# A two-layer hybrid decoder trunk: one plain group instead of three at the feed-forward's entry, two groups begun early, and other transfers at the start and the end

## The chip, the cores and the metric

The kernel runs on one core of a Trainium2 chip. The metric is the device time of one execution in microseconds (us), as the median of several runs. Before the change it is 2063.41 us (median of 3 runs, 2063.31 to 2064.4).

The core has five engines with a queue of instructions each: TensorE (PE) multiplies matrices, VectorE (DVE) and ScalarE (ACT) work on tiles, GpSimd (POOL) does elementwise work too, and SyncE (SP) issues transfers. An engine takes its queue strictly in the order in which the program was written out.

## What is computed

Two layers on a sequence of 1024 tokens with 1024 channels, all in float32. The feed-forward, where most of the change lies, is the second half of a layer:

```python
for l in range(DEPTH):
    h = rmsnorm(x, attn_norm[l])
    ...                                   # four token mixers on slices of h @ w_in[l]
    x = x + mixed @ w_o[l]
    h2 = rmsnorm(x, ffn_norm[l])
    gate, up = jnp.split(h2 @ w_gate_up[l], 2, axis=-1)
    x = x + (jax.nn.silu(gate) * up) @ w_down[l]
return rmsnorm(x, final_norm)
```

The inner width of the feed-forward is 2816, that is 22 groups of 128 gate columns and 128 up columns.

## The kernel before

**Products.** Activations are kept transposed, 128 channels by 512 tokens in a half tile (a "half" of a slot; two halves make a pair). The 1024 tokens are two halves, `HALVES = (1, 0)`. Each float32 operand is split into a high and a low part of type float32r: ACT copies the high part, DVE subtracts it (`split`, L281; `half_split`, L291; `pair_split`, L1114, on 1024 columns). A product of blocks is then three matmuls for each 128 channels: high by high, high by low, low by high (`mm3`, L267).

**The feed-forward.** Gate and up weights are one 2 by 2 block matrix for each group, the two token halves and the even and odd channel tiles the other. A plain group (`plain`, L1268) makes all eight products, four for each half `u`. A Strassen group makes seven, on combinations of the blocks: for the activations N1, N2, T3, T4 (`combine(j)`, L1054, for j = 0 to 3, made once for each layer), for the weights three sums that POOL makes (`GateUp.sums`, L1128) and a fourth (`sum4`, L1152). `GateUp(f)` (L1119) issues the two 512 KB loads of group `f`; `split1` to `split4` split its parts. `gu_start` (L1179) makes a Strassen group's first two products, on the blocks B11 and B21, which are plain parts of the input, and weights that are no sums. The other five need N2, N1, T3, B22 and T4 (`onto`, L1167, adds a product to a bank that holds one). `NPL = 3` groups are plain, 19 are Strassen groups (L1465 to L1535).

**The entry.** After the attention, `norm_a` (L1032) scales its outputs, `out_last(t, ma)` (L1084) adds the last quarter of the output projection for a token half, splits the result into B11 and B21 or B12 and B22, stores it and adds up its squares. `norm(u)` (L1423) makes the reciprocal root of a half's mean square (Ln, Exp and Square on ACT). The weights of groups 0 and 1 are loaded between the two halves of `out_last`. Then (L1426 to L1463) the six halves of plain groups alternate with the four calls of `combine`, the gates, silus and products of the plain groups, and the splits of group 3.

**The start and the end.** The parameters (`par`) are loaded by POOL (L131). `weights` (L203) loads a weight tile of 512 KB with SP and splits it. `enter(t)` (L362) loads x in blocks of 256 KB and splits each with a gain from `par`. At the end the last token half is finished in two passes of 256 columns: the last products, eviction (`evac`, L1566), sum of squares, `rnorm` (L326), and `finish` (L375), which multiplies by gain and norm in one DVE instruction and stores each of 8 tiles with SP (L384).

**The order.** The program text sets what depends on what. The order on each engine is then written out by a list scheduler (`arrange`, L1817) from estimated lengths (`length`, L1718) and a table of shifts (`MOVES`), which moves groups of instructions in rank; `order_engines` (L2015) fixes it. So a change of the text or of an estimate moves instructions in the whole program. PSUM banks have tags with fixed counts (`ps`, L177).

## Time and profile before

| | |
|---|---|
| median of 3 runs | 2063.41 us |
| the profiled execution's own time | 2062.8 us |
| its span, first to last instruction | 2061.0 us |
| mean granted clock of TensorE | 0.998 |
| DVE busy, share of the span | 75% |
| ACT busy | 47% |
| POOL busy | 28% |
| transferred | 289.76 MB, mean 141 GB/s |

A profile describes one execution. "Busy" is the time in which an engine worked; the groups give for each source line and operation the count, the busy time, the mean length of one in ns, and the idle time of the engine just before with what ended it ("<-DVE u L1050" is a DVE instruction on line 1050 that wrote a tile u). L272 is the helper that issues nearly all matmuls, L283 and L284 are the two halves of a split. Instructions of one engine overlap a little, so the lengths of instructions that follow each other add up to more than the time they take. The chain of waits follows the run back from its last instruction, at each step to what released it. A timeline row gives start, length and instruction, several alike as one row with a count.

### The profile page before, as it was taken

The numbers are of one execution on the slowest core, as the hardware profiler recorded it, in microseconds if no ns is written. First come the engines' busy times: TensorE is split into PE (matmuls) and PEld (weight loads), VectorE is DVE, ScalarE is ACT, GpSimd is POOL, SyncE is SP. The second block draws the span as 40 slices with busy tenths as digits, with TensorE's granted clock in tenths as the row PEclk, the third lists the DMA queues.
The fourth block names the chain that finished last, engine by engine and source line by source line (L and its number), as shares of the span: only waits on it lengthen the run. The fifth ranks groups of instructions, "written<-read, shape, count | busy, mean of one in ns | idle before, by whom it ended". The sixth has DMA issues, their size and how long they took to land.

```text
span 2061.0 us, 26301 instructions
## 1 busy us (share of the span) xinstructions
PE 2038.0 (99%) x9442; PEld 1680.9 (82%) x9442; DVE 1539.8 (75%) x2420; ACT 971.0 (47%) x1712; POOL 571.3 (28%) x453
## 2 busy tenths in 40 slices
PE   8999999999999999999999999999999999999997
PEld 6887888887888888888888878888888888888887
DVE  7888988976766767655656898878877677786555
ACT  7547556643333334444434576656433333354332
POOL 0000000047776775100000000000677677650000
PEclk9999999999999999999999999999999999999999
DMA  5110222324444446966411102233344444498652
GB/s 181 42 45 30 74 86 98 133 103 159 168 159 152 166 158 231 340 236 208 138 36 44 57 16 86 75 118 113 133 169 158 155 163 157 143 325 303 201 177 87
DMA packets 148819, 289.76 MB, mean 141 GB/s; under 512 B 12608, under 2 KB 72000, under 8 KB 148688
## 3 DMA queue, kind: packets, MB, share of 16 engines
q1 hardware_dynamic: 148656, 288.03, 40.5%
q8 instruction: 74, 1.21, 0.2%
q14 instruction: 57, 0.47, 0.1%
q0 software_dynamic: 32, 0.04, 0.0%
HBM read 204.66 MB, written 83.36 MB: 140 GB/s over the span
## 4 chain that ended last, share of the span: by engine, by line
PE 95%; DVE 2%; ACT 1%; DMA 1%; issue 1%; POOL 0%; DVEq 0%; SPq 0%; ACTq 0%; POOLq 0%
PE ps_mm L272 36%; PE ps_s L272 29%; PE ps_t L272 12%; PE ps_pv L272 8%; PE ps_pv L962 2%; PE ps_t L950 1%; PE ps_s L896 1%; PE ps_t L336 1%; PE ps_s L897 1%; PE ps_s L898 1%; PE ps_pv L572 1%; PE ps_mm L770 1%; PE ps_s L511 1%; DVE u L284 1%; PE ps_t L560 1%
## 5 line engine op out<-in xcount | busy, mean ns | idle before, releaser
L272 PE MATMUL ps_mm<-u,u 128*128 128x512 f32 (+1 forms) x3376 | 835.5, 389 | 1.4 <-DVE u L1001 1.2
L272 PEld LDWEIGHTS ps_mm<-u,u 128*128 128x128 f32 x3376 | 621.7, 188 | 126.6 <-issue 4.0
L272 PE MATMUL ps_s<-u,u 128*128 128x512 f32 x2672 | 636.0, 390 | 9.5 <-ACT u L286 7.4
L272 PEld LDWEIGHTS ps_s<-u,u 128*128 128x128 f32 x2672 | 501.6, 188 | 116.2 <-ACT u L286 7.4
L284 DVE TENSOR_TENSOR u<-u,u 128x1024 fp32r<-128x1024 f32 (+2 forms) x380 | 449.5, 1206 | 154.1 <-ACT u L283 118.9
L283 ACT CAST u<-u 128x1024 fp32r<-128x1024 f32 (+2 forms) x380 | 328.1, 888 | 480.4 <-PE ps_mm L272 192.8
L272 PE MATMUL ps_t<-u,u 128*128 128x512 f32 (+1 forms) x1212 | 284.1, 378 | 0.0
L272 PEld LDWEIGHTS ps_t<-u,u 128*128 128x128 f32 x1212 | 222.7, 188 | 43.0 <-issue 0.5
L959 POOL MEMSET u<- 128x128 f32 x32 | 5.9, 212 | 844.8 <-PE ps_mm L272 653.0
L1312 POOL TENSOR_TENSOR tp<-tp,u 128x512 f32<-128x512 f32 x88 | 144.1, 1639 | 231.6 <-ACT tp L1311 231.3
L161 POOL TENSOR_TENSOR u<-u 128x256 f32<-128x256 f32 x176 | 188.7, 1072 | 66.4 <-DVE u L284 30.5
L272 PE MATMUL ps_pv<-u,u 128*128 128x512 f32 x696 | 167.4, 389 | 0.4 <-ACT u L283 0.4
L272 PEld LDWEIGHTS ps_pv<-u,u 128*128 128x128 f32 x696 | 130.5, 188 | 28.1 <-ACT u L283 0.8
L1311 ACT ACTIVATE tp<-tp 128x512 f32<-128x512 f32 x88 | 55.5, 632 | 127.4 <-DVE tp L348 126.7
L1132 POOL TENSOR_TENSOR u<-u,u 128x512 f32<-128x512 f32 x38 | 66.9, 1761 | 140.9 <-ACT tp L1311 83.9
L286 ACT ACTIVATE u<-u,par 128x512 fp32r<-128x512 f32 x100 | 69.9, 717 | 58.0 <-DVE u L1577 18.6
L283 ACT CAST u<-ps_t 128x512 fp32r<-128x512 f32 (+4 forms) x136 | 65.1, 506 | 56.4 <-PE ps_t L950 32.5
L284 DVE TENSOR_TENSOR u<-ps_t,u 128x512 fp32r<-128x512 f32 (+4 forms) x136 | 76.9, 582 | 18.4 <-ACT u L283 17.6
L287 DVE SCALAR_TENSOR_TENSOR u<-u,par,u 128x512 fp32r<-128x512 f32 x100 | 72.7, 745 | 7.7 <-ACT u L286 7.5
L1524 DVE TENSOR_TENSOR tp<-ps_mm,tn 128x512 f32<-128x512 f32 x38 | 26.3, 691 | 61.5 <-PE ps_mm L272 61.5
L348 DVE TENSOR_TENSOR tp<-tp,u 128x512 f32<-128x512 f32 x76 | 69.0, 908 | 1.1
L318 ACT ACTIVATE tn<-u 128x512 f32<-128x512 f32 (+1 forms) x93 | 52.8, 589 | 31.8 <-DVE u L1577 28.4
(191 smaller groups left out, 2218.9 us busy)
## 6 DMA issues: line engine op xcount, KB each, us to landing
u<-in_w_gu SPq DMA_DIRECT2D x88, 512.0 KB, 4.3
ad<-u SPq DMA_DIRECT2D x154, 256.0 KB, 2.4
u<-ad SPq DMA_DIRECT2D x70, 512.0 KB, 5.4
u<-in_w_dn SPq DMA_DIRECT2D x68, 512.0 KB, 4.0
qd<-u SPq DMA_DIRECT2D x44, 512.0 KB, 2.9
u<-qd SPq DMA_DIRECT2D x32, 512.0 KB, 4.8
u<-in_w_in SPq DMA_DIRECT2D x30, 512.0 KB, 3.5
u<-in_xT SPq DMA_DIRECT2D x32, 256.0 KB, 5.1
```

The costliest lines, as they stand in the source:

```text
L161: pool.tensor_tensor(out=o, in0=o, in1=u, op=ALU.add)
L272: pe.matmul(o, w, r, start=start and k == 0 and i == 0, stop=stop and k == n - 1 and i == 2, skip_group_check=again,)
L283: act.copy(hi, f)
L284: dve.tensor_tensor(out=lo, in0=f, in1=rd(hi), op=ALU.subtract)
L286: act.activation(hi, f, AF.Copy, scale=gain)
L287: dve.scalar_tensor_tensor(out=lo, in0=f, scalar=gain, in1=rd(hi), op0=ALU.mult, op1=ALU.subtract)
L318: act.activation(q, f, AF.Square)
L348: dve.tensor_tensor(out=o, in0=a, in1=b, op=ALU.mult)
L962: pe.matmul(py[:, c0:], v_of(j, h), R.ap(s)[:, c0:], start=j == 0 and n == 0, stop=j == nj - 1 and n == 1,)
L1132: pool.tensor_tensor(out=F.ap(q + 1), in0=a21, in1=a22, op=ALU.add)
L1311: last_silu = act.activation(g, g, AF.Silu)
L1312: pool.tensor_tensor(out=g, in0=g, in1=r, op=ALU.mult)
```

## The change

- `NPL` is 1: one plain group, 21 Strassen groups.
- Group 0's loads are issued ahead of `norm_a(1)` and its split is written right behind it; group 1's loads, sums and first two splits follow, in between the attention's last steps. Group 2's loads take the place of the ones between the halves of `out_last`.
- Groups 1 and 2 are begun in the entry with `gu_start(..., early=True)`; their gate stands in a slot's half, and their first bank comes from the tag "s". The combinations are written between them. Group 3's loads are issued inside group 1, after its second weights are done.
- The silu of the plain group's first half is written ahead of the second `norm`.
- `par` is loaded by SP. The second weight tile of the program is loaded and split in two parts.
- In the last half's passes ACT multiplies by the gain (`gain`) ahead of the norm, DVE only by the norm, and ACT issues every second store.
- The scheduler's estimates for POOL, for DVE beside POOL, and for transfers issued by ACT are others, and all of `MOVES` is new.

```diff
@@ -39,7 +39,7 @@
 NSP = 3
 NG = NFF // 2
 
-NPL = 3
+NPL = 1
 
 PC_ATTN, PC_FFN, PC_MIX, PC_QN, PC_KVN, PC_CONV, PC_PS, PC_SINK = 0, 8, 16, 24, 26, 27, 33, 35
@@ -128,7 +128,7 @@
 
     par = cpool.tile([P, L * PC_N + NK], F32, name="par")
-    pool.dma_start(par, ins["params"])
+    sp.dma_start(par, ins["params"])
     cst = cpool.tile([P, CC_N], F32, name="cst")
     ident = cst[:, CC_ID : CC_ID + P]
     ones = cpool.tile([P, P], F32, name="ones")
@@ -200,11 +200,13 @@
         for i in ring.popleft():
             R.free_pair(i)
 
-    def weights(src, n):
+    def weights(src, n, parts=1):
+        cuts = [slice(i * n // parts, (i + 1) * n // parts) for i in range(parts)]
         if n > 2 * P:
             s = F.pair()
             raw = F.ap2(s)
-            sp.dma_start(raw[:, :n], src)
+            for c in cuts:
+                sp.dma_start(raw[:, c], src[:, c])
             hi, lo = (R.ap2(i) for i in ring_next())
             F.free_pair(s)
         else:
@@ -212,8 +214,9 @@
             sp.dma_start(raw[:, :n], src)
             hi = wpool.tile([P, 2 * P], F32R, name="vhi", tag="vhi")
             lo = wpool.tile([P, 2 * P], F32R, name="vlo", tag="vlo")
-        act.copy(hi[:, :n], raw[:, :n])
-        dve.tensor_tensor(out=lo[:, :n], in0=raw[:, :n], in1=rd(hi[:, :n]), op=ALU.subtract)
+        for c in cuts:
+            act.copy(hi[:, c], raw[:, c])
+            dve.tensor_tensor(out=lo[:, c], in0=raw[:, c], in1=rd(hi[:, c]), op=ALU.subtract)
         return hi, lo
 
     def rope_weights(l):
@@ -239,7 +242,7 @@
             if m is None:
                 expect(rope_weights, l)
             else:
-                expect(weights, ins["w_in"][l, m], 2 * HT)
+                expect(weights, ins["w_in"][l, m], 2 * HT, 2 if (l, m) == (0, 2) else 1)
         for d in range(NK):
             expect(weights, ins["w_o"][l, d, :, 2 * P :], 6 * P)
 
@@ -372,16 +375,23 @@
             F.free(xf[k][t])
         ratt[t] = ss.rnorm(t, parts=True)
 
-    def finish(x, t, cols):
+    def gain(x, d, t, cols):
+        a = F.ap(x[d][t])[:, cols]
+        act.activation(a, a, AF.Copy, scale=par[:, L * PC_N + d : L * PC_N + d + 1])
+
+    def finish(x, t, cols, gained=False):
 
         for d in range(NK):
             a = F.ap(x[d][t])[:, cols]
-            g = par[:, L * PC_N + d : L * PC_N + d + 1]
-            dve.scalar_tensor_tensor(
-                out=a, in0=a, scalar=g, in1=F.ap(ratt[t])[:, cols], op0=ALU.mult, op1=ALU.mult
-            )
+            if gained:
+                mul_to(a, a, F.ap(ratt[t])[:, cols])
+            else:
+                g = par[:, L * PC_N + d : L * PC_N + d + 1]
+                dve.scalar_tensor_tensor(
+                    out=a, in0=a, scalar=g, in1=F.ap(ratt[t])[:, cols], op0=ALU.mult, op1=ALU.mult
+                )
             o = out[d, :, t * HT : (t + 1) * HT]
-            sp.dma_start(o[:, cols], a)
+            (act if gained and d % 2 == 0 else sp).dma_start(o[:, cols], a)
 
     last_silu = None
     for l in range(L):
@@ -1176,15 +1186,16 @@
             act.copy(o, p)
             return o
 
-        def gu_start(w, between=None):
-
-            w.pa, pd = ps("aa"), ps("ad")
+        def gu_start(w, between=None, early=False):
+
+            w.pa, pd = ps("s" if early else "aa"), ps("ad")
             product(w.pa, blocks(w.s1, 0), hb[B11])
             k1 = snap(w.pa)
             if between:
                 between()
             product(pd, blocks(w.s2, 0), hb[B21])
-            w.gate = tmp("tp")
+            w.place = F.half() if early else None
+            w.gate = F.ap(w.place) if early else tmp("tp")
             dve.tensor_tensor(out=w.gate, in0=pd, in1=k1, op=ALU.add)
 
         steps = ((0, 0), (0, 1), (1, 0), (1, 1), (2, 0), (2, 1), (3, 1), (3, 0))
@@ -1244,23 +1255,27 @@
         for n in range(2):
             R.free(kb_[1][n][1])
             R.free(va[2 + n][1])
+        std = [GateUp(0)]
         ma1 = norm_a(1)
+        std[0].split_plain()
+        w = GateUp(1)
+        w.sums()
         mix_values(*prev)
         for n in range(2):
             R.free(kb_[1][n][0])
             R.free(va[n][1])
+        w.split1()
         ma0 = norm_a(0)
+        w.split2()
         out_some(len(parts))
         out_last(HALVES[0], ma1)
         while ring:
             ring_drop()
-        std = [GateUp(f) for f in range(2)]
-        std[0].split_plain()
+        wn = GateUp(2)
         out_last(HALVES[1], ma0)
         for pair in wa:
             for i in pair:
                 R.free_pair(i)
-        std[1].split_plain()
 
         acts = {f: [] for f in range(NPL)}
@@ -1268,7 +1283,7 @@
         def plain(f, u):
 
             w, b = std[f], ((B11, B21), (B12, B22))[u]
-            pg, pu = ps("wide"), ps("wide")
+            pg, pu = (ps("mm"), ps("mm")) if u == 0 else (ps("t"), ps("s"))
             product(pg, blocks(w.s1, 0), hb[b[0]], True, False)
             product(pg, blocks(w.s2, 0), hb[b[1]], False, True)
             product(pu, blocks(w.s2, 1), hb[b[0]], True, False)
@@ -1423,52 +1438,41 @@
         def norm(u):
             r2.append(F.ap(ss2.rnorm(HALVES[u], tag="pv", parts=True)))
 
-        std.append(GateUp(2))
         plain(0, 0)
         combine(0)
-        plain(1, 0)
         norm(0)
+        gu_start(w, early=True)
         combine(1)
         plain_gates()
+        plain_silus()
+        plain_acts()
+        norm(1)
         plain(0, 1)
-        norm(1)
-        plain_silus()
-        plain_gates()
-        combine(2)
-        plain_acts()
-        std[2].split_plain()
-        w = GateUp(3)
-        plain(1, 1)
-        plain_silus()
-        plain_gates()
-        w.sums()
-        combine(3)
-        plain_acts()
-        w.split1()
-        plain(2, 0)
-        plain_silus()
-        plain_gates()
-        w.split2()
-        plain_acts()
-        wn = GateUp(4)
-        plain(2, 1)
-        plain_silus()
-        plain_gates()
         for hl in hb[B12]:
             for i in hl:
                 R.free(i)
+        wn.sums()
+        wn.split1()
+        combine(2)
+        wn.split2()
+        gu_start(wn, early=True)
+        combine(3)
         w.split3()
-        plain_acts()
-        plain_silus()
+        plain_gates()
         w.sum4()
         w.split4()
+        plain_silus()
         plain_acts()
         for f in range(NPL, NFF):
-            if wn:
+            soon = f == NPL
+            if wn and not soon:
                 wn.sums()
-            wnn = GateUp(f + 2) if f + 2 < NFF else None
+            wnn = GateUp(f + 2) if f + 2 < NFF and not soon else None
             end = f == NFF - 1
-            gu_start(w, lambda: pending and second(*pending))
+            if f > NPL + 1:
+                gu_start(w, lambda: pending and second(*pending))
+            elif pending:
+                second(*pending)
             for g in [*range(NPL // 2 if f == NPL else 0), *range(f // 2, f // 2 + f % 2)]:
                 sp.dma_start(ad_of(B11, g), F.ap(acts[2 * g][HALVES.index(0)]))
             if f == NPL:
@@ -1480,7 +1484,7 @@
                 next(sums, None)
             gate = w.gate
             mul_to(gate, gate, r2[0])
-            if wn:
+            if wn and not soon:
                 wn.split1()
             if end:
                 used(B11, B21)
@@ -1488,8 +1492,10 @@
             onto(w.pa, blocks(w.s2, 1), hb[N2])
             for i in w.s2:
                 R.free_pair(i)
+            if soon:
+                wnn = GateUp(f + 2)
             k2 = snap(w.pa)
-            if wn:
+            if wn and not soon:
                 wn.split2()
             if end:
                 used(N2)
@@ -1528,6 +1534,8 @@
                 R.free_pair(i)
             acts[f] = [F.half()]
             neg_mul(F.ap(acts[f][0]), w.pa, gate)
+            if w.place is not None:
+                F.free(w.place)
             if wn:
                 wn.split4()
             pending = f, gate1, up
@@ -1647,8 +1655,10 @@
                     finish(x, 0, whole)
                 evac(B22, m, p, cols)
                 ss.add(1, F.ap(x[2 * m][1])[:, cols], cols)
+                for d in (2 * m, 2 * m + 1):
+                    gain(x, d, 1, cols)
             ratt[1] = ss.rnorm(1, cols, tag="s")
-            finish(x, 1, cols)
+            finish(x, 1, cols, True)
 
@@ -1719,7 +1729,7 @@
     n = max(width(a) for a in ins + outs)
     ps = any(a.bass_ap.tensor.name.startswith("ps_") for a in ins)
     if eng == "POOL":
-        return 206 if kind == "InstMemset" else 230 + 2.07 * n
+        return 206 if kind == "InstMemset" else 1150 + 0.5 * n
     if eng == "ACT":
         if kind == "InstTensorCopy":
             return 157 + 0.84 * n if ps else 187 + 0.845 * n
@@ -1772,9 +1782,12 @@
                 v.size *= int(n)
             if eng == "POOL":
                 v.ns, v.tail = 700, 4200
+            elif eng == "ACT":
+                v.ns, v.tail = 450, 2400
         else:
             v.ns = length(eng, kind, i, ins, outs)
-            v.onchip = not any(a.bass_ap.tensor.name.startswith("ps_") for a in ins + outs)
+            if not any(a.bass_ap.tensor.name.startswith("ps_") for a in ins + outs):
+                v.onchip = 0.7 if kind == "InstTensorScalarPtr" and len(ins) < 3 else 0.4
             if ins:
                 v.rows = tuple(areas(a)[1][0][0] for a in (ins[0], outs[0]))
             if eng == "ACT" and len(outs) > 1:
@@ -1915,7 +1928,7 @@
                 if rows != v.rows and (rows[1] or v.rows[0]):
                     t = max(t, end + SHIFT[e])
             if e == "DVE" and v.onchip:
-                ns += 0.8 * sum(max(0.0, min(b, t + ns) - max(a, t)) for a, b in pool_busy[-8:])
+                ns += v.onchip * sum(max(0.0, min(b, t + ns) - max(a, t)) for a, b in pool_busy[-8:])
             if v.table and v.table != table:
                 table = v.table
                 ns += 1280
@@ -1948,54 +1961,55 @@
     return out
 MOVES = {
...
```

2 lines of the change are left out of this document (1 added, 1 removed), and 97 rows, old and new, of the table MOVES.

## The prediction, made before the changed kernel ran

> **What bounds the kernel now.** I read the busy table first, then the chain of waits, then TensorE's waits, then the windows by stage.
>
> ```profile
> span 2061.0 us, 26301 instructions
> PE 2038.0 (99%) x9442; PEld 1680.9 (82%) x9442; DVE 1539.8 (75%) x2420; ACT 971.0 (47%) x1712; POOL 571.3 (28%) x453
> ...
> PE 95%; DVE 2%; ACT 1%; DMA 1%; issue 1%; POOL 0%; DVEq 0%; SPq 0%; ACTq 0%; POOLq 0%
> ```
>
> TensorE (PE) is busy for 99% of the span and holds 95% of the chain that ended last. So matmuls that go away shorten the run, as long as PE stays fed. Its visible waits are few; the longest four:
>
> ```profile
> PE ps_s L272 <- ACT u L286: 7.4, 1, 7.4
> PE ps_s L336 <- DVE u L320: 1.4, 1, 1.4
> PE ps_mm L272 <- DVE u L1001: 1.2, 1, 1.2
> PE ps_s L272 <- DVE te L1512: 1.0, 1, 1.0
> ```
>
> The first is the start, the second the end, the third lies ahead of layer 1's feed-forward, the fourth in layer 0's entry. The windows show who feeds PE there (columns: window and its length, then busy time and count of PE, PEld, DVE, ACT, POOL, the clock, the DMA share, GB/s):
>
> ```profile
> 400.00:480.00 80.00, 78.54 (x345) 64.20 (x344) 63.68 (x77) 35.67 (x54) 35.81 (x23) 1.00 0.30 103
> ...
> 1380.00:1400.00 20.00, 18.80 (x83) 15.15 (x82) 16.77 (x25) 13.17 (x19) 0.00 (x0) 1.00 0.47 157
> 1400.00:1420.00 20.00, 20.00 (x90) 16.57 (x89) 20.00 (x32) 13.19 (x24) 0.00 (x0) 1.00 0.42 160
> 1420.00:1440.00 20.00, 20.00 (x90) 16.52 (x89) 16.89 (x28) 12.26 (x21) 0.00 (x0) 1.00 0.00 1
> ```
>
> At the entry PE loses 1.46 us of 80 in layer 0 and 1.20 us in layer 1, 2.7 us in all, and VectorE (DVE) is full for 20 us of 20 in one window. So DVE is the next bound, there and only there.
>
> **Part 1: fewer products.** A product of two blocks is 12 matmuls of 128x512, 2.72 / 12 = 0.2267 us each:
>
> ```profile
> 504.42 2.72 PE ps_pv L272 x12
> 507.14 2.72 PE ps_mm L272 x12
> ```
>
> A plain group makes 8 such products, a Strassen group 7. Two groups in each of two layers change over: 4 products, 48 matmuls. The built programs bear this out: 9,421 matmuls before, 9,373 after, all the missing ones 128x512 (the page counts 9,442 records). 4 x 2.72 = **10.9 us** less PE work, on the path wherever PE is the bound.
>
> **Part 2: the entry with less cover.** Before, three plain groups (3 x 8 x 2.72 = 65.3 us) ran while DVE and ScalarE (ACT) made the combinations N1, N2, T3, T4. Now PE has one plain group (21.8 us) and four products of the two groups begun early (10.9 us), 32.7 us in all, half the cover. The work that it hides isn't halved. I listed both queues as built and summed them with row durations. DVE issues overlap, so I take its pitch from starts that follow each other:
>
> ```profile
> 1405.11 0.69 DVE L324 TENSOR_TENSOR u<-u,tn 128x512 f32<-128x512 f32 x1
> 1405.71 0.75 DVE L287 SCALAR_TENSOR_TENSOR u<-u,par,u 128x512 fp32r<-128x512 f32 x1
> 1406.38 0.69 DVE L324 TENSOR_TENSOR u<-u,tn 128x512 f32<-128x512 f32 x1
> ...
> 1413.29 1.22 DVE L284 TENSOR_TENSOR u<-u,u 128x1024 fp32r<-128x1024 f32 x1
> 1414.42 0.74 DVE L287 SCALAR_TENSOR_TENSOR u<-u,par,u 128x512 fp32r<-128x512 f32 x1
> ```
>
> 0.60 us for two tensors of 512, 0.66 with a gain, 1.13 for a split of 1024. In layer 1, from the last output-projection result to the last N2 block that group 1 needs, DVE has 35 instructions: 26 x 0.60 + 6 x 0.66 + 3 x 1.13 = 22.9 us. PE has 101 matmuls between the same points: 101 x 0.2267 = 22.9 us. There is no margin. In layer 0 the tightest place is the second split of group 2's weights: DVE 33.1 us against PE 35.4 us, 2.2 us of margin.
>
> This holds while GpSimd (POOL) rests. Group 2's three sums, one silu product and one fourth sum fall in the same stretch:
>
> ```profile
> L1050 DVE SCALAR_TENSOR_TENSOR u<-u,u 128x512 f32<-128x512 f32 x44 | 51.8, 1178 | 0.7
> L1312 POOL TENSOR_TENSOR tp<-tp,u 128x512 f32<-128x512 f32 x88 | 144.1, 1639 | 231.6 <-ACT tp L1311 231.3
> L1132 POOL TENSOR_TENSOR u<-u,u 128x512 f32<-128x512 f32 x38 | 66.9, 1761 | 140.9 <-ACT tp L1311 83.9 <-PE ps_s L272 38.3 <-PE ps_pv L272 10.8
> L1154 POOL TENSOR_TENSOR u<-u 128x512 f32<-128x512 f32 x38 | 64.9, 1709 | 9.3 <-DVE u L284 9.3
> L1134 POOL TENSOR_TENSOR u<-u,u 128x512 f32<-128x512 f32 x38 | 53.3, 1403 | 2.8
> L1133 POOL TENSOR_TENSOR u<-u,u 128x512 f32<-128x512 f32 x38 | 51.7, 1361 | 0.0
> ```
>
> The same kind of DVE instruction that takes 0.69 us alone takes 1.18 us on average in the groups, where POOL works: some 0.49 us lost per 1.1 us of shared time. POOL has 1.76 + 1.36 + 1.40 + 1.64 + 1.71 = 7.9 us of work here, so DVE loses at most 7.9 x 0.49 / 1.1 = 3.5 us. That makes PE wait 3.5 us in layer 1 and 3.5 - 2.2 = 1.3 us in layer 0.
>
> ACT also has less room, because the program as built has six more table loads (11 for 5), three per entry: silu of the plain group's first half, then Ln and Exp of the second norm, then silu again. A load as the trace has it:
>
> ```profile
> 1443.73 0.63 ACT L339 ACTIVATE tn<-tn 128x512 f32<-128x512 f32 x1
> 1444.38 1.28 ACT L1311 ACT_TABLE_LOAD   x1
> 1445.68 0.63 ACT L1311 ACTIVATE tp<-tp 128x512 f32<-128x512 f32 x1
> ```
>
> From the end at 1444.36 to the next start it costs 1.32 us. Three are 4.0 us more of ACT per entry, which had 13.2 of 20 us busy in its fullest window. Between the copy of group 1's first product and the N2 cast, ACT's queue as built holds 17 instructions, two loads among them: 2 x 1.28 and 15 casts, copies and activations of 0.5 to 1.0 us, about 11.4 us, against 52 matmuls, 11.8 us. It fits alone. Casts and splits of one combination hand over from DVE to ACT and back, so a late DVE pulls ACT along; for that I add 1 us per layer. [...]
>
> The weight splits moved ahead of the output projection (two for group 0, two for group 1: 4 x 1.13 us of DVE, 4 x 1.05 us of ACT per layer) go into a stretch that still has room:
>
> ```profile
> 300.00:400.00 100.00, 99.82 (x491) 82.08 (x490) 89.10 (x184) 68.01 (x138) 1.04 (x6) 1.00 0.34 121
> ```
>
> 10.9 us of 100 are free on DVE there. They can still delay a softmax split that PE wants next; I take 0.5 us per layer. The 512 KB weight loads for them go up SP's queue past output weights and saved partial sums, at 0.33 us an issue; the DMA share of 0.34 leaves room, so nothing for that. New waits at the entry: 3.5 + 1.3 + 2 x 1 + 2 x 0.5 = 7.8 us. Of the old 2.7 us I count all as gone, since their places are reordered: **5.1 us net**. The bounds: nothing new (-2.7), and every one of the 26 short instructions at the contended price, 26 x 0.49 = 12.7 us a layer (25.4 - 2.7 = +22.7).
>
> **Part 3: the start.** The parameters no longer go through POOL but as the third transfer on SP, behind 768 KB of weights, and another 256 KB goes ahead of x.
>
> ```profile
> DMA packets 2099, 5.02 MB, mean 314 GB/s; under 512 B 238, under 2 KB 238, under 8 KB 2099
> ...
> 1.26 5.37 DMA par<-in_params
> ...
> 5.60 0.63 ACT L313 ACTIVATE u<-u 128x512 f32<-128x512 f32 x1 [0.18 <-DMA u<-in_xT]
> ...
> 0.00:10.00 10.00, 2.57 (x5) 1.78 (x6) 4.35 (x10) 6.30 (x8) 0.90 (x5) 1.00 0.79 262
> 10.00:20.00 10.00, 10.00 (x43) 8.17 (x42) 9.97 (x17) 10.00 (x19) 0.00 (x0) 1.00 1.04 399
> 20.00:30.00 10.00, 10.00 (x45) 8.24 (x44) 9.03 (x14) 8.09 (x14) 0.00 (x0) 1.00 0.58 207
> 30.00:45.00 15.00, 15.00 (x67) 12.39 (x67) 10.56 (x16) 9.56 (x17) 0.00 (x0) 1.00 0.14 44
> ```
>
> Today the first product starts at 7.4 us, 0.8 us after the parameters land at 6.63; x is there at 5.60. With 555 KB more ahead of it, x lands 1.4 (at the 399 GB/s of 10 to 20 us) to 1.8 us later (at the mean of 314), at 7.0 to 7.4, and the first product starts 0.3 to 0.8 us later. After the start PE now loses 45 - 7.4 - 160 x 0.2267 = 1.3 us up to 45 us, waiting for the second weight; that one will be split before x comes, so this goes. Net **-0.8 us**, between -1.0 and +0.8 if the stall stays.
>
> **Part 4: the end.** In the last pass ACT multiplies by the gain early (8 instructions, in time in which it now waits), DVE's last multiplications have no scalar, and every second store is issued by ACT.
>
> ```profile
> 2051.82 0.38 ACT L338 ACTIVATE tn<-ps_s 128x256 f32<-128x256 f32 x1 [1.31 <-PE ps_s L336]
> ...
> 2054.12 3.26 DVE L380 SCALAR_TENSOR_TENSOR u<-u,par,u 128x256 f32<-128x256 f32 x8
> ...
> L384 SPq DMA_DIRECT2D out<-u x24: 332/388/408, 2026.6 to 2058.0; - x24
> ...
> L380 DVE SCALAR_TENSOR_TENSOR u<-u,par,u 128x256 f32<-128x256 f32 x16 | 6.5, 479 | 0.1
> L324 DVE TENSOR_TENSOR u<-u,tn 128x256 f32<-128x256 f32 x12 | 4.8, 420 | 0.6 <-ACT tn L318 0.5
> ```
>
> Eight multiplications at 420 for 479 ns: -0.5 us. The last store is issued at 2058.0, 0.6 us after the last multiplication (2057.4), because eight issues of 0.39 us stand in one queue; with two queues that goes. The one gain that comes after the last eviction hides in ACT's 1.31 us wait; without that cover it costs 0.4 to 0.5 us. An issue by ACT isn't in this trace: I price it as SP's, with 0.2 us off for doubt. **-0.9 us**.
>
> The planner's shifts (MOVES) are all new, so order changes everywhere. In the groups PE is full before and after. For the attention stages I take 0, within 3 us either way: a window like 300 to 400 shows 0.18 us of visible wait, but matmul records overlap and hide shorter ones.
>
> **Sum:** -10.9 + 5.1 - 0.8 - 0.9 = -7.5 us. The profiled execution took 2062.8 us (span 2061.0 and 1.8 around it), so 2055.3; the median, 2063.41, is 0.6 above it: **2055.9**, and I say 2055.5.
>
> **Rivals.**
> 1. *The cover holds.* The sums of POOL run before the stretch, DVE keeps 0.60 us, and the old waits go: -10.9 - 2.7 - 1.7 = -15.3, some 2048. For it: layer 0's margin. Against: layer 1 has none.
> 2. *The entry takes the gain back.* DVE at half the contended loss, 6.4 us a layer, with hand-overs of 2 us each: 16.8 - 2.7 - 12.6 = +1.5 at worst, 2060 to 2065. For it: DVE full for 20 us; against: POOL has only 7.9 us to disturb it with.
> 3. *Slower.* The N2 products of groups 1 and 2 stand next to each other in PE's queue, with nothing to run instead. If DVE meets the contended price throughout, PE waits 12.7 us a layer: 25.4 - 2.7 - 12.6 = +10.1, 2073. It decides from 7.6 us of wait a layer. Against: POOL would have to work through all 23 us.
> 4. *Table loads are dearer than the row.* If a pause as long as the load itself, 1.28 us, stood behind each, three a layer, ACT would fall 3.8 us behind PE in each: 2055.5 + 7.6 = 2063. The trace has no such pause. [...]
> 5. *The new order elsewhere costs what the matmuls save*, so that the change doesn't do what it says: 2063. Nothing in the trace speaks for it.
>
> **How the numbers follow.** Forecast 0.60 (alone 2051 to 2059); rival 1 0.19; rival 2 0.08; rival 3 0.07; rivals 4 and 5 0.03 each. A measurement of this kernel can tell about 0.2% (4.1 us) from no change. Faster (below 2059.3): 0.60 + 0.19 and a little of rival 2, 0.80; slower (above 2067.5): 0.07; same: 0.13. The range takes in rival 1 down to 2047 and leaves out most of 2 to 5: 2047 to 2061.5.
>
> **What would show it.** Right: 48 matmuls fewer; PE's waits at 430 to 460 and 1410 to 1440 us grow to some 4 us each, released by DVE's differences and splits or ACT's casts; first product at 7.7 to 8.2 us with no gap behind; tail from the last matmul to the last landing about 1 us shorter; table loads of 1.28 us with nothing behind them. Wrong: waits of 8 us or more a layer there (rival 3), none at all (rival 1), or PE waits in attention that weren't there.

## The result, and the profile after

The changed kernel takes **2086.05 us** (median of 4 runs, 2085.22 to 2087.59); the kernel before took 2063.9 us beside it (4 runs). The ratio is 1.0105, with a 95% interval of 1.0093 to 1.0117: **1% slower**, some 22 us, where I had forecast 8 us faster. The profiled execution took 2085.22 us, with a span of 2083.3.

The page of the kernel after, its busy table and its chain:

```profile
span 2083.3 us, 26357 instructions
...
PE 2037.0 (98%) x9394; PEld 1673.2 (80%) x9394; DVE 1555.6 (75%) x2441; ACT 996.0 (48%) x1755; POOL 596.9 (29%) x468
...
PE 76%; DVE 10%; POOL 6%; issue 4%; DMA 2%; ACT 2%; SPq 0%; DVEq 0%; POOLq 0%; ACTq 0%
```

There are 48 matmul records fewer (9,394 for 9,442), as intended. But the chain that ended last is no longer PE alone: 95% has become 76%, and DVE and POOL hold 16% of it. PE is still busy for 98% of its span, which shows how little that share says: a matmul's record (389 to 391 ns in the mean on ps_mm and ps_s) is longer than its place in the queue (0.2267 us from one start to the next for 128x512), so short waits hide in it.

TensorE's waits in the kernel after (sum, times, longest):

```profile
PE ps_mm L275 <- ACT tn L1186: 10.3, 13, 1.1
PE ps_s L275 <- ACT u L289: 8.8, 1, 8.8
PE ps_mm L275 <- DVE u L287: 4.7, 2, 2.7
PE ps_s L275 <- ACT tn L1186: 3.3, 2, 2.3
PE ps_mm L275 <- ACT u L218: 3.0, 2, 1.6
PE ps_mm L275 <- DVE u L1109: 1.9, 2, 1.0
```

The first row is new, and there are 13 of it: they stand in the loop over the groups. The windows of the loops, before and after:

```profile
540.00:800.00 260.00, 260.00 (x1149) 215.29 (x1148) 180.83 (x179) 88.27 (x122) 184.15 (x136) 1.00 0.46 162
1500.00:1800.00 300.00, 300.00 (x1324) 248.32 (x1323) 211.38 (x206) 104.06 (x144) 211.79 (x158) 1.00 0.44 154
```

```profile
400.00:480.00 80.00, 75.64 (x319) 60.01 (x319) 70.33 (x85) 44.84 (x67) 39.94 (x29) 0.98 0.34 117
...
540.00:800.00 260.00, 252.26 (x1105) 206.51 (x1104) 175.88 (x175) 86.20 (x120) 176.28 (x133) 1.00 0.42 149
...
1500.00:1800.00 300.00, 294.06 (x1288) 240.64 (x1287) 208.45 (x202) 99.47 (x140) 213.20 (x156) 1.00 0.47 161
```

PE, full before, loses 7.74 us of 260 and 5.94 of 300 visibly, and 44 and 36 matmuls are missing from the same windows. At the entry (400 to 480 us) it loses 4.36 us instead of 1.46, and the mean clock is 0.98 instead of 1.00.

To sum short waits too, I went through the starts of all matmuls: the distance from one start to the next, less the usual distance of that shape (0.2267 us for 128x512). What is left is PE's loss, in us, by stage (counted from the first product on; the entry runs from the first sum of the output projection's last quarter to the twelfth group from the end, the loop over the last twelve):

| stage | before | after | g1 | h2 | k6 |
|---|---|---|---|---|---|
| start and attention, layer 0 | 10.2 | 12.9 | 11.5 | 11.7 | 10.2 |
| entry, layer 0 | 4.0 | 13.4 | 11.4 | 7.7 | 5.9 |
| loop, layer 0 | -0.3 | 4.6 | -0.2 | 4.5 | -0.1 |
| down-projection 0, attention 1 | 6.7 | 7.6 | 7.4 | 8.1 | 7.6 |
| entry, layer 1 | 1.4 | 10.3 | 10.6 | 4.9 | 4.9 |
| loop, layer 1 | -0.3 | 4.7 | 0.2 | 4.8 | 0.2 |
| down-projection 1 | 1.4 | 1.4 | 1.4 | 1.4 | 1.4 |
| sum | 23.0 | 54.8 | 42.2 | 43.1 | 30.2 |

After minus before is 31.8 us; less the 10.9 us of matmuls saved, that is 20.9 of the 22.3 by which the span grew. The first product also starts 1.4 us later, and the end takes 0.5 us less, so the sum closes to 0.5 us. **The entries cost 18.3 us more, the loops 9.9, start and attention 3.6.** The last three columns are experiments.

### The profile page after: what moved, and what is told of

The parts are those of the page before. It is cut to its first block, busy times and chain, and to the rows that moved or that the text cites. A ratio compares the mean times of both kernels' runs of the same rounds, so it can differ in the third digit from the quotient of the medians.

```text
span 2083.3 us, 26357 instructions
## 1 busy us (share of the span) xinstructions
PE 2037.0 (98%) x9394; PEld 1673.2 (80%) x9394; DVE 1555.6 (75%) x2441; ACT 996.0 (48%) x1755; POOL 596.9 (29%) x468
## 4 chain that ended last, share of the span: by engine, by line
PE 76%; DVE 10%; POOL 6%; issue 4%; DMA 2%; ACT 2%; SPq 0%; DVEq 0%; POOLq 0%; ACTq 0%
PE ps_mm L275 31%; PE ps_s L275 21%; PE ps_t L275 9%; PE ps_pv L275 6%; DVE u L287 3%; POOL u L161 2%; PE ps_pv L972 2%; PE ps_t L960 1%; POOL u L1143 1%; POOL tp L1327 1%; POOL u L1164 1%; DVE u L290 1%; PE ps_s L906 1%; PE ps_pv L582 1%; PE ps_t L339 1%
## 5 line engine op out<-in xcount | busy, mean ns | idle before, releaser
L275 PE MATMUL ps_mm<-u,u 128*128 128x512 f32 (+1 forms) x3426 | 854.0, 389 | 22.1 <-ACT tn L1186 10.3
L275 PE MATMUL ps_s<-u,u 128*128 128x512 f32 x2676 | 663.7, 391 | 12.3 <-ACT u L289 8.8
L286 ACT CAST u<-u 128x1024 fp32r<-128x1024 f32 (+2 forms) x388 | 335.8, 888 | 414.3 <-PE ps_s L275 71.1
L275 PE MATMUL ps_t<-u,u 128*128 128x512 f32 (+1 forms) x1118 | 263.1, 378 | 0.5 <-DVE u L287 0.5
L275 PEld LDWEIGHTS ps_t<-u,u 128*128 128x128 f32 x1118 | 201.3, 188 | 40.2 <-DVE u L287 1.3
L1327 POOL TENSOR_TENSOR tp<-tp,u 128x512 f32<-128x512 f32 x84 | 134.5, 1601 | 187.5 <-ACT tp L1326 187.1
L1142 POOL TENSOR_TENSOR u<-u,u 128x512 f32<-128x512 f32 x42 | 56.8, 1352 | 152.0 <-PE ps_s L275 46.8
L1164 POOL TENSOR_TENSOR u<-u 128x512 f32<-128x512 f32 x42 | 77.7, 1849 | 37.7 <-DVE u L287 23.1
L351 DVE TENSOR_TENSOR tp<-tp,u 128x512 f32<-128x512 f32 x80 | 77.3, 966 | 2.5
L1143 POOL TENSOR_TENSOR u<-u,u 128x512 f32<-128x512 f32 x42 | 73.0, 1739 | 0.0
```

The source lines that it names most:

```text
L275: pe.matmul(o, w, r, start=start and k == 0 and i == 0, stop=stop and k == n - 1 and i == 2, skip_group_check=again,)
L286: act.copy(hi, f)
L351: dve.tensor_tensor(out=o, in0=a, in1=b, op=ALU.mult)
L1142: pool.tensor_tensor(out=F.ap(q + 1), in0=a21, in1=a22, op=ALU.add)
L1143: pool.tensor_tensor(out=F.ap(q), in0=a21, in1=a11, op=ALU.add)
L1164: pool.tensor_tensor(out=q4, in0=q4, in1=F.ap(self.raw[1] + 1), op=ALU.add)
```

## The experiments

All medians stand beside the kernel before, whose own median was 2063.2 to 2064.0 us each time. The results at a glance, with the ratio to the kernel before and its 95% interval:

| run | us | ratio |
|---|---|---|
| e1 after, old estimates | 2076.62 | 1.0061 (1.0046 to 1.0076) |
| e2 before, new estimates | 2067.61 | 1.0016 (1.0007 to 1.0026) |
| e3 after, no shifts | 2114.28 | 1.0244 (1.0229 to 1.0259) |
| e4 before, no shifts | 2078.12 | 1.0066 (1.0049 to 1.0083) |
| g1 after, copies first on ACT | 2072.45 | 1.0044 (1.0028 to 1.0061) |
| g2 after, one split first on DVE | 2083.30 | 1.0097 (1.0082 to 1.0112) |
| g3 both and old start | 2071.67 | 1.0041 (1.0026 to 1.0056) |
| g4 after, old start | 2083.78 | 1.0099 (1.0083 to 1.0114) |
| h1 g1, combinations later | 2077.31 | 1.0065 (1.0049 to 1.0082) |
| h2 after, POOL emptied at the entry | 2074.38 | 1.0052 (1.0037 to 1.0067) |
| h3 h1, more copies first | 2079.30 | 1.0074 (1.0059 to 1.0089) |
| h5 before, new end | 2063.34 | 0.9995 (0.9986 to 1.0004) |
| k1 only the pieces emptied | 2082.10 | 1.0089 (1.0074 to 1.0104) |
| k2 only the groups' sums emptied | 2077.92 | 1.0071 (1.0056 to 1.0086) |
| k3 pieces later | 2086.97 | 1.0112 (1.0095 to 1.0129) |
| k4 planner with DVE's loss as measured | 2088.83 | 1.0125 (1.0110 to 1.0140) |
| k5 k3 with its shifts put right | 2072.54 | 1.0039 (1.0025 to 1.0053) |
| k6 h2 and g1 together | 2063.34 | 0.9999 (0.9990 to 1.0008) |

### Estimates, shifts or text? (e1 to e4)

```diff
-        return 206 if kind == "InstMemset" else 1150 + 0.5 * n
+        return 206 if kind == "InstMemset" else 230 + 2.07 * n
-                v.onchip = 0.7 if kind == "InstTensorScalarPtr" and len(ins) < 3 else 0.4
+                v.onchip = 0.8
```

Expected of e1:

> The kernel after, with the planner's two estimates set back (POOL 230 + 2.07 n, on-chip loss of 0.8). Its shifts and everything else stay. Theory 1: the new estimates put POOL's fourth sum and silu product too late in the loop over the groups. Then the loop goes back to about 38.1 us for two groups (after: 39.3), PE fills the windows 540 to 800 us, and the time is 2058 to 2064. Theory 2: the loop is late because the new text starts it with loads and sums behind. Then the loop stays at 39.3 us for two groups and the time is 2083 to 2089.

Expected of e2, the opposite exchange in the kernel before:

> The kernel before, with the new estimates (POOL 1150 + 0.5 n, on-chip loss of 0.7 and 0.4) and nothing else. The order as built differs little on PE (some 50 lines), on POOL in 86 lines. Theory 1 (the new estimates cost what is lost): two groups take over 39 us instead of 38.08 and the time is 2080 to 2090. Theory 2 (the new text costs it): PE stays full in the loop, 2062 to 2066.

Expected of e3 (MOVES = {}):

> The kernel after with MOVES empty: the planner's order without the hand-made shifts. Theories 1 and 2 both put the loop's loss outside the shifts (none names a group of the first layer's loop), so the loop stays at about 39.3 us for two groups and PE goes on losing some 8 us in 540 to 800 us. A third theory, that the new shifts push the loop's entry into a bad state, expects the loop to come back to 38.1 us. The attention stages, which have most shifts, get longer by an amount that none of them gives; I guess 5 to 30 us in all.

Expected of e4 (MOVES = {} in the kernel before):

> The kernel before with MOVES empty. What its shifts are worth without the rest of the change: by the first theory and the second the loop stays full (38.1 us for two groups) and only the attention and the two entries get longer, by the same 5 to 30 us as in the kernel after. If here too the loop loses, the loop's state hangs on how it is entered, and the third theory gains.

In e1 the loop came back, to 38.1 us for two groups, as the first theory says, but the time fell only to 2076.6 and not to 2058 to 2064: counted as in the table, its entries still lose 25 us. In e2 the loop stayed full and the kernel lost 3.6 us. So neither theory holds alone: the new estimates (these two; those for transfers issued by ACT were not set back) spoil the loop only together with the new text. By the starts of each group's sum te (one a group), a group takes 19.04 us in the kernel before; in the kernel after 20.53 and 18.77 us in turn, 39.3 for two; in e1 20.55 and 17.55, which is the full rate. The loop without shifts loses just as much (e3), so the third theory falls. The shifts are worth 14 us in the kernel before and 28 us in the kernel after.

### The loop: what stands ahead of the copy (g1)

One stall of the loop in the kernel after, on ACT, POOL and PE (start, length, line, operation; in brackets the idle time ahead and what ended it):

```profile
608.88 0.57 ACT L1186 COPY tn<-ps_s 128x512 f32<-128x512 f32 x1
612.44 0.62 ACT L286 CAST u<-u 128x512 fp32r<-128x512 f32 x1 [2.99 <-POOL u L1164]
612.96 0.58 ACT L1186 COPY tn<-ps_mm 128x512 f32<-128x512 f32 x1
...
610.13 2.27 POOL L1164 TENSOR_TENSOR u<-u 128x512 f32<-128x512 f32 x1
...
609.80 2.88 PE L275 MATMUL ps_s<-u,u 128*128 128x512 f32 x12
613.60 2.58 PE L275 MATMUL ps_mm<-u,u 128*128 128x512 f32 x10 [0.91 <-ACT tn L1186]
```

Read it backwards. PE's product in ps_mm starts when ACT's copy of the same bank ends, at 613.54 us. The copy could have gone 3 us earlier, right behind the copy of ps_s, when its product was finished; it stands behind the cast of a fourth sum, which waits 2.99 us for POOL. The cast itself is for a later product. ACT kept the order of its queue: it stood idle for 2.99 us ahead of the cast and did not take the copy first. So a cast that nobody misses held up a copy that PE waits for. In the order as built, such a cast stands right ahead of the copy in 15 places, of which the swap takes 13; in e1 in 3 (and in 3 with either of the two old estimates alone), in the kernel before in none.

```diff
+        for a, b in zip(range(len(queue)), range(1, len(queue))):
+            if queue[a].ins[0].name in MARK["s4"] and queue[b].ins[0].name in MARK["k5"]:
+                queue[a], queue[b] = queue[b], queue[a]
```

> The kernel after, its order kept as it is on PE, DVE, POOL and SP; on ACT alone, where the cast of a fourth sum (split4) stands right ahead of the copy of the fifth product (snap, k5), the two change places: 13 places. Theory A: the loop's stall of 1.07 us in every second group comes from ACT's queue: PE may write into that bank again only after the copy, and the copy stands behind a cast that waits for POOL's fourth sum. Then those stalls go, two groups take 38.1 us instead of 39.3, and the time is 2074 to 2079. Theory B: DVE and POOL are too slow for the pair whatever stands first. Then another wait takes the stall's place in the next product: 2083 to 2088.

Measured: 2072.45 us. The same place in g1:

```profile
607.17 0.58 ACT L1187 COPY tn<-ps_s 128x512 f32<-128x512 f32 x1
608.29 0.59 ACT L1187 COPY tn<-ps_mm 128x512 f32<-128x512 f32 x1 [0.54 <-PE ps_mm L275]
610.73 0.62 ACT L286 CAST u<-u 128x512 fp32r<-128x512 f32 x1 [1.84 <-POOL u L1164]
...
608.10 2.88 PE L275 MATMUL ps_s<-u,u 128*128 128x512 f32 x12
610.82 2.88 PE L275 MATMUL ps_mm<-u,u 128*128 128x512 f32 x12
```

The copy goes as soon as its product is done, the cast waits as before, and PE goes on without a gap. Two groups take 38.1 us; the loops' loss is gone (table). Theory A holds for the loop: 13 swaps on one engine bring back 9.3 us there. The rest of the 13.6 us by which the median fell lies, by the table, in the start and layer 0's entry; whether the swap brought it was not tried.

### The entry: DVE and POOL in turns (g2, h1, h3, h2)

The stall of layer 0's entry in the kernel after: DVE, POOL, PE.

```profile
449.78 1.77 DVE L1060 SCALAR_TENSOR_TENSOR u<-u,u 128x512 f32<-128x512 f32 x1
451.48 1.78 DVE L1320 SCALAR_TENSOR_TENSOR u<-te,tp 128x512 f32<-128x512 f32 x1
453.30 1.67 DVE L1060 SCALAR_TENSOR_TENSOR u<-u,u 128x512 f32<-128x512 f32 x1
454.89 2.28 DVE L287 TENSOR_TENSOR u<-u,u 128x1024 fp32r<-128x1024 f32 x1
...
451.09 1.62 POOL L1144 TENSOR_TENSOR u<-u,u 128x512 f32<-128x512 f32 x1
452.67 1.74 POOL L1142 TENSOR_TENSOR u<-u,u 128x512 f32<-128x512 f32 x1
454.38 1.71 POOL L1143 TENSOR_TENSOR u<-u,u 128x512 f32<-128x512 f32 x1
...
457.23 0.97 PE L275 MATMUL ps_mm<-u,u 128*128 128x512 f32 x3 [2.73 <-DVE u L287]
```

Three instructions on DVE (two combinations of the plain pair and a product), 0.68 us alone, take 1.7 us each beside POOL's sums. The ends tell how: POOL's end at 452.71, DVE's at 453.26, POOL's at 454.41, DVE's at 454.97. Each finishes 0.55 (DVE) or 1.15 us (POOL) after the other: they take turns. The split that PE waits for is queued behind two such instructions. It doesn't wait for POOL itself: ACT's cast of the same sum was done at 452.09 us, 2.8 us before the split began. Two ways to test it: change DVE's order, or empty POOL.

```diff
+        for k in range(2, len(queue)):
+            if queue[k].ins[0].name in MARK["q"] and queue[k - 1].ins[0].name in MARK["combo"]:
+                queue.insert(k - 2, queue.pop(k))
```

> The kernel after, its order kept on PE, ACT, POOL and SP; on DVE alone, once in each layer, the split of group 2's sum tile (third split, 128x1024) goes ahead of the second half's product and of the last combination T4 of the plain pair, which now stand ahead of it beside POOL at 1.7 us each. Theory A: the entry's largest stall (2.9 us at 454 us, 2.1 us at 1483 us, each with 3.4 us of half clock behind it, 1.7 us more) is those two instructions in DVE's queue. Then both stalls and both stretches of half clock go: 2077 to 2080. Theory B: DVE is full in the entry, so what stands behind is late instead: gain below 3 us, 2083 to 2088.

Measured: 2083.3 us, 2.7 less than after. The split came in time, and PE then waited 2.6 us on DVE's next instruction, the sum te (L1518 in the kernel after), which frees its bank. So h1, on top of g1, put these two instructions behind four others:

```diff
-                queue.insert(k - 2, queue.pop(k))
+                queue[k - 2 : k + 4] = queue[k : k + 4] + queue[k - 2 : k]
```

> The kernel of the copies (g1) and one thing more: once in each layer the two instructions that stood ahead of the split in g2 (the second half's product and the combination T4 of the plain pair) go behind the sum up, the sum gate1 and its product too. In g2 PE waited on the next of these instead. Theory A (DVE's order: the two stand ahead of four that PE waits for): both stalls of some 3 us at the entry go, with the half clock where there is any: 2072.5 - 2.9 - 3.0 - 1.7 = 2064 to 2067. Theory B (DVE has no time left in the entry; what goes later makes the stores of the combinations and the loads behind them on SP late): the wait turns up again within the next two groups, 2070 to 2075.

Measured: 2077.31 us, 4.9 *more* than g1. PE's longest wait at layer 0's entry, SP's queue and the casts in h1:

```profile
PE ps_s L275 <- ACT u L286: 3.2, 1, 3.2
```

```profile
447.73 11.09 SPq L1344 DMA_DIRECT2D ad<-u  x5
...
459.89 1.99 ACT L286 CAST u<-u 128x1024 fp32r<-128x1024 f32 x2 [8.49 <-DMA ad<-u]
```

The stores of the combinations hold SP for 11.09 us, since the last of them wait for the instructions that were put later. The casts that PE waits for had to wait for these stores to land ("<-DMA ad<-u") and come late instead. In the kernel after the same five stores held SP for 6.87 us. The wait turned up again, as theory B says, but by way of the stores and not of the loads behind them, and it cost 2 us more than B's 2070 to 2075.

h3 added, on ACT, the copy k2 ahead of silu and a cast, 33 places:

```diff
+        for k in range(2, len(queue)):
+            if [queue[k + n - 2].ins[0].name in MARK[m] for n, m in enumerate(("silu", "qa", "k2"))] == [True] * 3:
+                queue.insert(k - 2, queue.pop(k))
```

> The kernel h1 and one thing more: wherever ACT's queue has silu, the cast of the sum tile and then the copy of the running product (snap, k2), the copy goes first (33 places). After and g1 lose 2.43 us at 547 us and 1.2 us in layer 1 at a T3 product that waits for this copy, while silu ahead of it waits for DVE. Theory A: these go, 3 us less than h1, 2061 to 2064, about the kernel before. Theory B: silu comes later everywhere by one copy (0.6 us) and POOL's products with it: no gain against h1 or a loss.

Measured: 2079.3 us, 2 more than h1. The stalls near 547 us went, others came (2.1 us in layer 1). Each of these moves only moved the stall.

h2 left the order and took POOL's work away, so it leaves out part of the computation:

```diff
+                    if 1 < self.f < 4 and o is not a21:
+                        FULL[pool.memset(o, 0.0).ins.name] = HT
+                        continue
...
+                e = slice(0, 8 if c < 3 * n else n)
+                FULL[pool.tensor_tensor(out=o[:, e], in0=o[:, e], in1=u[:, e], op=ALU.add).ins.name] = n
```

> The kernel after, with POOL nearly emptied in the entry: of the three sums of groups 2 and 3, two are filled with zeros and the third done over 8 columns, and the first three pieces of the down-projection's sums are done over 8 columns; the planner still counts them in full, so that the order stays (PE the same, DVE 10 lines, ACT 5). Part of the computation is left out in this way. If POOL's work beside DVE is what stretches DVE's instructions at 448 to 457 us from 0.68 to 1.77 us, these come back to 0.7 to 0.8, the stalls of 2.9 and 2.1 us and their half clock go, and the time is 2077 to 2080. If DVE's amount of work is the limit whatever POOL does, the stalls keep more than half of their length: 2083 to 2087. In both the loop's stalls of 1.07 us stay.

Measured: 2074.38 us, 11.7 less than after and more than I expected. The same instructions on DVE in h2:

```profile
445.27 0.68 DVE L1346 TENSOR_TENSOR u<-u 128x512 f32<-128x512 f32 x1
445.87 0.68 DVE L1064 SCALAR_TENSOR_TENSOR u<-u,u 128x512 f32<-128x512 f32 x1
446.48 0.68 DVE L1328 SCALAR_TENSOR_TENSOR u<-te,tp 128x512 f32<-128x512 f32 x1
447.19 0.69 DVE L1064 SCALAR_TENSOR_TENSOR u<-u,u 128x512 f32<-128x512 f32 x1
```

The entry's window (length, then busy time and count of PE, PEld, DVE, ACT, POOL, then clock, DMA share, GB/s), in the kernel after and in h2:

```profile
437.60:458.30 20.70, 17.97 (x80) 14.53 (x79) 20.63 (x19) 7.81 (x12) 20.32 (x13) 1.00 0.64 231
```

```profile
437.60:458.30 20.70, 20.58 (x91) 16.75 (x90) 17.85 (x20) 7.16 (x10) 13.87 (x14) 1.00 0.88 292
```

In the kernel after DVE and POOL are both full for 20.7 us, and PE isn't. With POOL at 13.87 us DVE has 2.85 us to spare and PE is full. The entries' loss falls from 23.7 to 12.6 us (table), and the stretches of half clock are gone: the mean clock is 1.00 in 400 to 480 and in 1400 to 1500 us, where the kernel after has 0.98 in both. So POOL's work in the entry is shown as the cause of 11.1 of the 18.3 us that the entries lose more. In the stall above it acts by stretching DVE's instructions, which are the same in both kernels; elsewhere h2 also has the sums ready earlier, and the runs don't part the two. Of the 7.2 us left, 2.3 are a wait near 547 us for a copy on ACT, in h2 as in the kernel after (the row of 3.3 above); the rest stays open.

### Which of POOL's work, and can it be put elsewhere? (k1 to k6)

k1 keeps only the second half of h2's edit, k2 only the first; both leave out part of the computation.

> The kernel after with only the first three pieces of the down-projection's sums emptied on POOL (12 additions a layer, done over 8 columns instead of 256, counted in full by the planner: the order is the same on PE, DVE, ACT and SP). Part of the computation is left out. h2 emptied these and the sums of groups 2 and 3, and gained 11.7 us. If the pieces, which the new entry lets start at 437 us, are what holds DVE up, 6 to 10 of these us come back here: 2076 to 2080. If it is the groups' own sums, at most 4: 2082 to 2086.

> The other half of h2: only the sums of groups 2 and 3 are emptied on POOL (two filled with zeros, the third over 8 columns), the pieces of the down-projection's sums stay. Part of the computation is left out. If the groups' sums are what holds DVE up at the entry, 6 to 10 us of h2's 11.7 come back: 2076 to 2080. If it is the pieces, at most 4: 2082 to 2086. If k1 and k2 each gain nearly all or nearly nothing, the cost is a matter of overlap, and not of one of them.

Measured: k1 gains 4.0 us, k2 8.1; together 12.1, h2's 11.7. Two thirds are the groups' own sums, which can't be left out.

k3 starts the pieces, the other third, with group 3, and has g1's swap and the old start:

```diff
-            if not end:
+            if not end and f > NPL + 1:
                 next(sums, None)
```

> A kernel that computes everything: the copies first as in g1, the old start, and the pieces of the down-projection's sums begun with group 3 instead of group 1, so that POOL is freer in the entry; the planner orders the groups anew, the attention stages keep their order. If the pieces matter, 2072.5 - 1.5 - 4 to 8 = 2063 to 2067; if not, about 2071.

Measured: 2086.97 us. Its entries lose 18 us instead of g1's 22, but layer 1's attention loses 25.0 instead of 7.4: the shifts are stored by the number of a group of instructions, and with pieces issued later the numbers move by two. k5 has the same text and each shift on its old group:

> The kernel k3 with its shifts put right. In k3 the groups of instructions are numbered anew, since pieces are issued later, and from layer 0's loop on every shift fell on another group (two further on in layer 1's attention); there k3 lost 17.6 us more than g1 and 2 us less at the two entries. Here the shifts stand on the groups they were made for. If that was k3's loss, layer 1's attention comes back to what g1 has and the entries keep their gain: 2067 to 2071, a little below g1 (2072.5) and above the kernel before. If the attention of layer 1 suffers from the later pieces themselves, it stays at 2080 to 2088.

Measured: 2072.54 us (five runs, 2066.89 to 2073.28); layer 1's attention is back at 7.2. That settles k3. It is above the 2067 to 2071 expected. The later pieces are worth next to nothing: the entries lose 20.2 us, for 22.0 in g1, the stalls stand elsewhere, and the time is g1's, though k5 has the old start as well.

k4 gives the planner the loss that the trace shows (`v.onchip = 1.6`), with g1's swap and the old start:

> A kernel that computes everything: the copies first as in g1, the old start, and in the planner the loss of DVE beside POOL as the trace shows it (0.68 us become 1.77: a loss of 1.6 of the overlap with the undisturbed length, where after has 0.4 and before 0.8). If the entry is slow because the planner underrates this loss, it now puts the combinations where POOL rests, and the time is 2062 to 2067. If there is no room for them at all with one plain group, it stays at 2069 to 2073.

Measured: 2088.83 us, above both ranges. The loop went to an even 19.04 us a group, but the entries lost 31 us and the attention stages 9 more than g1's; the shifts were made for other estimates, and which part is theirs stays open.

k6 joins h2 and g1:

> h2 (POOL emptied in the entry; part of the computation left out) and g1 (the copies first on ACT) in one kernel. If the two causes are separate, entry and loop, their gains add up: 2086.05 - 11.7 - 9 to 13.6 = 2061 to 2065, and PE's loss from the output projection to the end of the loop falls from some 33 us in the kernel after to about 12. If they are one cause, much less: 2069 to 2073.

Measured: 2063.34 us, the time of the kernel before. The sum of the single gains is 11.7 + 13.6 = 25.3; together they give 22.7. So the two causes are separate, and together as large as the 22 us by which the kernel after is slower. They aren't all that the change costs: k6 still loses 7.2 us more than the kernel before (table), and its first product starts 2.1 us later (9.55 us). That takes back most of the 10.9 us of matmuls saved, and so even with that work of POOL left out the change only draws level.

### Start and end (g3, g4, h5)

g4 puts the old start back; g3 has that, g1 and g2.

```diff
-    sp.dma_start(par, ins["params"])
+    pool.dma_start(par, ins["params"])
...
-                expect(weights, ins["w_in"][l, m], 2 * HT, 2 if (l, m) == (0, 2) else 1)
+                expect(weights, ins["w_in"][l, m], 2 * HT)
```

> The kernel after with the start of before alone: parameters through POOL's queue, the first weight loaded and split in one piece. The order elsewhere stays the same (34 matmuls differ in place, all at the start). By the two traces the new start costs 1.4 us (first product at 8.79 us instead of 7.43) and the 12 us behind it nothing: the first product comes back to 7.4 us and the time is 2084 to 2086. My prediction's step (the second weight's stall goes with the new start, a gain of 0.8) expects 2086 to 2088 here.

> Both moves at once, and the start as in the kernel before (parameters through POOL's queue, the first weight in one piece). If the three parts simply add up, theory A gives 2086 - 9 - 7 - 1.4 = 2068 to 2071; theory B (waits that move elsewhere) 2080 to 2086.

Measured: g4 2083.78, 2.3 us less than after; g3 2071.67, 0.8 less than g1, which the medians can't tell apart, though the single gains of g2 and g4 add up to 5: the parts don't add, and which is lost was not tried. First products start at 8.11 and 8.04 us, not at 7.4.

h5 is the kernel before with the new end (gain and finish as in the change's diff):

> The kernel before with the new end alone (gain multiplied early on ACT, last products without a scalar, every second store issued by ACT). My prediction's step: 0.9 us less from the last eviction to the end, 2062.3; the trace of after against before says 0.4 to 0.5 us, 2062.7. The medians can hardly tell these apart; the profile can: the time from the last matmul to the last landing.

Measured: 2063.34, ratio 0.9995 (0.9986 to 1.0004): no difference that the medians can tell. From the last two matmuls to the end of the span it takes 9.23 us for 9.98: 0.75 less, between the 0.9 of my step and the 0.5 of the kernel after.

## Why the prediction was wrong

**Part 1 was right**: 48 records fewer, 10.9 us, and the account by stages closes with it to 0.5 us.

**Part 2 failed in its size, by 13 us.** I had 5.1 us net; the entries lose 23.7 us for 5.4, 18.3 net. The step that failed is "DVE loses at most 7.9 x 0.49 / 1.1 = 3.5 us". Both factors were too small. The 0.49 came from a mean (1178 ns over 44 instructions, of which many met no work on POOL); beside a full POOL an instruction loses 1.1 us (1.77 for 0.68). That price stood in the trace before, as the longest of the 44 (shortest, median, longest in ns):

```profile
L1050 DVE SCALAR_TENSOR_TENSOR u<-u,u x44: 677/1219/1781, 457.6 to 1845.3; 128x512 f32<-128x512 f32 x44
```

And POOL's 7.9 us counted only one group's sums: in 20.7 us at the entry it works 20.32, since the next group's sums, the first pieces of the down-projection's sums and the silu products of the plain group fall there too. Rival 3 named this mechanism ("DVE meets the contended price throughout"); against it I wrote that POOL would have to work all the time, and it does. I also held the order of the wait for settled: a late split. The runs show a chain through three queues (DVE's combinations, SP's stores of them, ACT's casts that wait for the stores), and of the moves on DVE g2 gained 2.7 us and h1 lost 4.9.

The table loads did what I had priced:

```profile
427.20 0.71 ACT L1071 ACTIVATE te<-u,par 128x512 f32<-128x512 f32 x1
427.91 1.28 ACT L1326 ACT_TABLE_LOAD   x1
429.21 0.63 ACT L1326 ACTIVATE u<-u 128x512 f32<-128x512 f32 x1
```

1.28 us, with the next instruction 0.02 us behind; rival 4 falls.

**"In the groups PE is full before and after" failed**, for 9.9 us. I had put the new order elsewhere at 0 for lack of a sign against it (rival 5, chance 0.03). The order as built was there to be read: 15 casts right ahead of a copy that PE waits for, none before. I compared numbers of instructions there, and not who stands behind whom.

**Part 3 failed in sign**: g4 prices the new start at 2.3 us, where I had a gain of 0.8. The first product starts at 8.79 us instead of 7.43, later than the 7.7 to 8.2 foreseen, and what I took for a wait for the second weight isn't one. The term that was too small is the landing of x: 2.4 us later (8.02 for 5.60) instead of 1.4 to 1.8. The start of the kernel after, ACT's first instruction on x, PE's first rows and two windows:

```profile
8.02 0.72 ACT L289 ACTIVATE u<-u,par 128x512 fp32r<-128x512 f32 x1 [0.32 <-DMA u<-in_xT]
...
8.79 0.80 PE L275 MATMUL ps_s<-u,u 128*128 128x512 f32 x1 [8.79 <-ACT u L289]
9.39 0.63 PE L275 MATMUL ps_mm<-u,u 128*128 128x512 f32 x1
```

```profile
10.00:20.00 10.00, 10.00 (x36) 7.99 (x35) 9.90 (x15) 10.00 (x17) 0.00 (x0) 1.00 1.03 400
20.00:30.00 10.00, 10.00 (x45) 8.25 (x45) 7.62 (x12) 6.39 (x12) 0.00 (x0) 1.00 0.54 206
```

PE is busy without a gap and yet runs 36 matmuls in the first of these windows instead of the 44 that 0.2267 us each would give: its first matmuls stand 0.427 us apart, nearly twice as far, until 14.5 us (until 10.9 us in the kernel before), though the column of the clock says 1.00 (the traces hold no record of the clock ahead of 14.62 and 10.89 us). In each of the six kernels whose first 45 us I summed, PE is busy there for longer than its matmuls take at 0.2267 us each: 2.0 us in the kernel before, 2.9 in the kernel after, 1.7, 2.6, 3.4 and 2.8 in e1 to e4. The start differs between kernels by more than this edit: over all profiles the first product starts at 6.88 to 7.43 us in kernels with the text of before, at 7.99 to 8.21 with the changed text and the old start, and at 8.79 to 10.13 with the new start and the shifts.

**Part 4 was half right.** The end, in the kernel after:

```profile
2073.81 0.70 PE L339 MATMUL ps_s<-u,ones 128*128 128x256 f32 x2 [1.42 <-DVE u L323]
...
2076.84 2.77 DVE L351 TENSOR_TENSOR u<-u,u 128x256 f32<-128x256 f32 x8
...
2078.31 1.86 ACTq L394 DMA_DIRECT2D out<-u  x4
...
2077.30 2.01 SPq L394 DMA_DIRECT2D out<-u  x4
```

Eight multiplications take 2.77 us for 3.26: the 0.5 us foreseen. In this profile the second queue gave nothing: from the last multiplication (2079.61) to the end of the span it takes 3.7 us, as before (3.6), although the last issue is done earlier. From 2073.81 to the end it takes 9.49 us for 9.98, 0.5 less instead of 0.9. In h5 it was 0.75, so what the second queue is worth stays open within some 0.3 us.

**The attention stages.** The stages outside entry and loop lose 3.6 us more; 1.0 of it is the longer slow start (counted up to 45 us), the rest lies within the 3 us allowed. But the row of 3.0 us among TensorE's waits was a sign of being wrong that I had named, PE waits in attention that weren't there: 1.6 us in layer 0 and 1.4 in layer 1, where the kernel before has 0.2 in all. PE waits for the cast of an output weight, and the cast waits for its load:

```profile
336.17 0.83 ACT L218 CAST u<-u 128x768 fp32r<-128x768 f32 x1 [2.75 <-DMA u<-in_w_o]
```

I had put 0.5 us a layer on the splits moved into this stretch and nothing on the moved loads. Whether those loads make this one late was not tried.

**Left open:** why the planner comes to the bad order only with the new text and both new estimates together, and whether an order tuned anew for one plain group could do better than g1. No run keeps three plain groups and takes the rest of the change. None of the versions tried is faster than the kernel before.

## What to carry to other kernels

A stage that hides work behind matmuls has a budget on every engine beside which the one you counted gets slower (here POOL, beside which DVE's 0.68 us became 1.77): sum POOL's work in the same stretch before you halve the cover, and price an instruction beside it by the worst row (1.78 us here), not by the mean (1.18). When a scheduler makes the order, compare for each engine what stands directly ahead of the instruction that TensorE waits for; a copy behind a cast that waited for a third engine cost 1.07 us here in every second group. And adjustments that are stored by position fall on other instructions as soon as the text ahead of them changes (k3 against k5: 14 us).
